# The experts' weights split into two parts one megabyte at a time

## The chip, the core and the metric

The kernel runs on one core of a Trainium2 chip. The metric is the device time of one execution in microseconds, as the median of several runs. TensorE multiplies, ScalarE (ACT) and VectorE (DVE) do element-wise work, GpSimd (POOL) a little of it, and SyncE (SP) issues most DMA transfers. Each engine works through its own instructions in a fixed order and waits on semaphores for the others.

## What is computed

A model of several layers runs over 256 tokens of 1024 channels, all in float32. The change touches only its last layer, a mixture of experts. A router picks two of eight experts for each token, and each expert is a gated feed-forward network.

```python
gates = jnp.sum(jax.nn.one_hot(top_idx, N_EXPERTS, dtype=jnp.float32) * top_w[..., None], axis=1)
for e in range(N_EXPERTS):
    y = swiglu_2(t, w_gate[e], w_up[e], w_down[e])       # (silu(t @ w_gate) * (t @ w_up)) @ w_down
    out = out + gates[:, e:e + 1] * y
```

The hidden width of an expert is 3584, so its three matrices hold 11 million weights, 44 MB. All eight hold 352 MB.

## The kernel before

TensorE takes the weights in a rounded 32-bit format, and one rounded copy is not exact enough. So every weight tile is split: ACT copies the raw float32 tile to `hi` in the rounded format (line 337), and DVE subtracts `hi` from the raw tile and writes the rest to `lo` (line 338). Each product is then made of matmuls with `hi` and matmuls with `lo`. The function `halves` does this for a tile of 128 partitions x 1024 columns (512 KB), which `load_half` has fetched (line 326, on SP's queue). All layers use it: the feed-forward, mixer and delta-net layers ahead of the experts get their weights through `stream`, and the experts call `chunk`, which handles two such tiles, 1 MB.

`hi` and `lo` come from two pools of three buffers each. A writer that wants a buffer waits until every reader of the tile that lay in it three tiles earlier is done: for `hi` that is DVE and TensorE, for `lo` TensorE. In the experts' stage the raw tiles rotate through four pools (`rawb`, `rawc`, `raw`, `rawe`) with 8 + 12 + 4 + 3 = 27 buffers of 512 KB. A few more buffers (`rawd`, `rawf`) serve once at the beginning, and the first eight tiles are fetched ahead, while the delta-net layer still computes. SP issues a transfer as soon as DVE has released the tile that lay in its buffer.

The function `short` runs the experts. A step is one of the seven blocks of 512 hidden columns of one expert, so there are 8 x 7 = 56 steps of six chunks. `gate_up` multiplies two chunks of gate weights and two of up weights, then makes silu times up (`sl`, line 1930 on ACT and 1931 on DVE). `down` of the step before multiplies two chunks of down weights after its own small matmuls (`x<-BOTH,sl`) and a split of their result (`hh`). For experts with at most 64 tokens (`FEW`), the high and the low part of the tokens lie side by side in one operand. They need two matmuls for each tile of 128 x 512 weights, eight in a chunk, and two extra matmuls a step that add the two sides (`gu<-both,BOTH`). The two experts with more tokens need three, twelve in a chunk. Six experts are of the first kind (42 steps), two of the second (14 steps: they run from about 1970 to 2090 us and from 2320 to 2430 us). Once an expert, `scatter` adds its output to the result (`yh`, `yl`, `ACC`), and `gather` collects the tokens of the next one or two experts (`XG`).

An automatic scheduler fixes the order on each engine when the kernel is built, from priorities in program order and its own estimate of times.

Of the kernel before, what the change touches and what calls it, by code (L numbers as in the profile page):

```python
# [9 lines left out]
F32 = mybir.dt.float32  # L10
# [47 lines left out]
NRB, NRC, NRD, NRE, NRF = 8, 12, 3, 3, 1  # L58
# [9 lines left out]
def _const_arrays():  # L68
# [31 lines left out]
    add("zero", np.zeros((P, P)))  # L100
# [149 lines left out]
class _K:  # L250
# [63 lines left out]
    def raw(self):  # L314
        if self.once:
            return self.T(self.once.pop(0), [P, 1024], "raw")
        self.nraw += 1
        return self.T(self.rawp[self.nraw % len(self.rawp)], [P, 1024], "raw")

    def load_half(self, ap, j, parts=1):  # L320
        if self.ahead:
            return self.ahead.pop(0)
        raw = self.raw()
        n = 1024 // parts
        for i in range(parts):
            self.nc.sync.dma_start(raw[:, i * n:i * n + n], ap[j, :, i * n:i * n + n])
        return raw

    def halves(self, raw, parts=1):

        nc = self.nc
        hi = self.T(self.hip, [P, 1024], "hi", F32R)
        lo = self.T(self.lop, [P, 1024], "lo", F32R)
        n = 1024 // parts
        for i in range(parts):
            c = slice(i * n, i * n + n)
            nc.scalar.activation(hi[:, c], raw[:, c], AF.Copy)  # L337
            nc.vector.tensor_tensor(lo[:, c], raw[:, c], hi[:, c].bitcast(F32), OP.subtract)  # L338
        return hi, lo
# [918 lines left out]
    def deltanet(self, outer):  # L1258
# [9 lines left out]
        with ExitStack() as st:  # L1268
# [158 lines left out]
            def feed():  # L1427
                for part, hg in _DN_ORDER:
                    yield from {"k": keys, "v": values, "z": zs}[part](hg)
                while not {("i", 0), ("i", 1)} <= done:  # L1430
                    yield 1.0

                first.close()
                self.ringb = outer.enter_context(tc.tile_pool(name="rawb", bufs=NRB, side="right"))
                self.once = [self.ringb] * NRB
                ahead.extend([self.load_half(self.A["moe"][0][j // 2], j % 2) for j in range(NRB)])
# [280 lines left out]
    def experts(self, base, HH, HL, ACC, RS, GT, key, st):  # L1717
# [50 lines left out]
        def gate_up(e, fb, XG, RX):  # L1768
            gu = []
            for m in range(2):  # L1770
                ps = self.T(self.psg, [P, 512], "gu")
                for q in range(2):
                    ch = self.chunk(self.A["moe"][e][fb * 6 + m * 2 + q])
                    for kk in range(4):
                        k = q * 4 + kk
                        wh, wl = ch[kk // 2]
                        c = slice((kk % 2) * 512, (kk % 2) * 512 + 512)
                        xh, xl = XG[:, 0, k, :], XG[:, 1, k, :]
                        self.mm(ps, ps, xh, wh[:, c], k == 0, False)
                        self.mm(ps, ps, xl, wh[:, c], False, False)  # L1780
                        self.mm(ps, ps, xh, wl[:, c], False, k == DT - 1)
                gu.append(ps)
# [5 lines left out]
        def down(e, fb, sl, ya, OT):  # L1788
# [6 lines left out]
            end = (e, fb) == (NE - 1, 6)  # L1795
            if end:
                raws = [self.load_half(self.A["moe"][e][fb * 6 + 4 + j // 2], j % 2, 2) for j in range(4)]
                self.gb, self.fin = self.raw(), self.raw()
                nc.sync.dma_start(self.gb, self.A["prow"][:, 24:24 + D].partition_broadcast(P))
            for n in range(2):  # L1800
                if not end:
                    ch = self.chunk(self.A["moe"][e][fb * 6 + 4 + n])
                for i in range(4):
                    c = slice((i % 2) * 512, (i % 2) * 512 + 512)
                    first, last = fb == 0 and i == 0, fb == 6 and i == 3
                    if end and i % 2 == 0:
                        w = self.halves(raws[2 * n + i // 2], 2)
                    wh, wl = w if end else ch[i // 2]
                    self.mm(ya[n], ya[n], hh[:, i, :], wh[:, c], first, False)
                    self.mm(ya[n], ya[n], hl[:, i, :], wh[:, c], False, False)  # L1810
                    self.mm(ya[n], ya[n], hh[:, i, :], wl[:, c], False, last)
# [31 lines left out]
    def short(self, HH, HL, ACC, RS, keyp, keyl, GTp, BOTH, where, st):  # L1843
# [16 lines left out]
        def gather(es):  # L1860
# [3 lines left out]
            for t in range(2):  # L1864
                for u, e in enumerate(es):
                    nc.vector.tensor_scalar(OH[:, t, u, :], self.c("iota"), keyp[:, t, e:e + 1], None, OP.is_equal)
                    nc.vector.tensor_scalar(OL[:, t, u, :], self.c("iota") if FEW[e] else self.c("zero"),
                                            keyl[:, t, e:e + 1] if FEW[e] else 1.0, None, OP.is_equal)
# [40 lines left out]
        def gate_up(e, fb, XG, RX):  # L1909
            gu = []  # L1910
            for m in range(2):
                ps = self.T(self.psg, [P, 512], "gu")
                for q in range(2):
                    ch = self.chunk(where(e)[fb * 6 + m * 2 + q])
                    for kk in range(4):
                        k = q * 4 + kk
                        wh, wl = ch[kk // 2]
                        c = slice((kk % 2) * 512, (kk % 2) * 512 + 512)
                        self.mm(ps, ps, XG[:, 0, k, :], wh[:, c], k == 0, False)
                        if not FEW[e]:  # L1920
                            self.mm(ps, ps, XG[:, 1, k, :], wh[:, c], False, False)
                        self.mm(ps, ps, XG[:, 0, k, :], wl[:, c], False, k == DT - 1)
# [11 lines left out]
        def down(e, fb, sl, ya, OT):  # L1934
# [13 lines left out]
            end = (e, fb) == (NE - 1, 6)  # L1948
            if end:
                raws = [self.load_half(where(e)[fb * 6 + 4 + j // 2], j % 2, 2) for j in range(4)]  # L1950
                self.gb, self.fin = self.raw(), self.raw()
                nc.sync.dma_start(self.gb, self.A["prow"][:, 24:24 + D].partition_broadcast(P))
            for n in range(2):
                if not end:
                    ch = self.chunk(where(e)[fb * 6 + 4 + n])
                for i in range(4):
                    c = slice((i % 2) * 512, (i % 2) * 512 + 512)
                    first, last = fb == 0 and i == 0, fb == 6 and i == 3
                    if end and i % 2 == 0:
                        w = self.halves(raws[2 * n + i // 2], 2)  # L1960
                    wh, wl = w if end else ch[i // 2]
                    self.mm(ya[n], ya[n], hh[:, i, :], wh[:, c], first, False)
                    if not FEW[e]:
                        self.mm(ya[n], ya[n], hl[:, i, :], wh[:, c], False, False)
                    self.mm(ya[n], ya[n], hh[:, i, :], wl[:, c], False, last)
# [94 lines left out]
    def build(self):  # L2060
        nc, tc = self.nc, self.tc
        with ExitStack() as st:
# [7 lines left out]
            ring = pool("raw", 4, side="right")  # L2070
            self.nraw, self.rawp, self.once, self.ahead = -1, [ring], [], []
            self.hip = pool("hi", 3, side="right")
            self.lop = pool("lo", 3, side="right")
# [56 lines left out]
            ringe = pool("rawe", NRE)  # L2130
            self.nraw, self.rawp = -1, [ringb] * NRB + [ringc] * NRC + [ring] * 4 + [ringe] * NRE
            self.once, self.ahead = rest + [ring] * 4 + [ringe] * NRE, ahead
# [21 lines left out]
```

## Time and profile before

| | us |
|---|---|
| median of 3 runs | 2569.28 (2568.91 to 2570.13) |
| profiled execution, its own time | 2570.35 |
| its span, first to last instruction | 2568.6 |
| DVE lo (line 338), all 1128 | 1344.0 busy, mean 1221 ns |
| ACT hi (line 337), all 1128 | 1167.7 busy, mean 1054 ns |
| DMA in the span | 603 MB, mean 235 GB/s |

Busy time of an instruction in the rows runs from its start to its end. On DVE and ACT the next one can start a little before the end of the one in front, so the cost of one among many is the distance from start to start. A matmul takes 0.39 us from start to end where the next one starts 0.23 us later. In a row of the timeline, several instructions of one kind are merged; the bracket gives the idle time of the engine before them and what ended it.

### The profile page before, as it was taken

What the parts mean: (1) busy time and instruction counts of PE and PEld (TensorE: products, weight loads), DVE (VectorE), ACT (ScalarE), POOL (GpSimd) and SP (SyncE); (2) the same over time, 40 slices, a digit from 0 to 9 for tenths busy, and PEclk for the clock granted to TensorE, in tenths of its full rate; (3) what the DMA queues carried; (4) which work ended last, traced back from release to release, by engine and by line L of the source; (5) the groups of instructions that cost most, each with busy time, mean ns of one, the idle gap of its engine ahead of it and who ended that gap; (6) DMA issues with size and microseconds to landing.
All of it is one profiled execution on the core that took longest, in us unless ns stands there. A gap on an engine that the chain in (4) does not pass through costs nothing. (4 is left out here: it accounts for less than half of the span.)

```text
span 2568.6 us, 44854 instructions
## 1 busy us (share of the span) xinstructions
PE 2499.9 (97%) x16795; PEld 2195.2 (85%) x16795; DVE 1981.9 (77%) x2663; ACT 1615.1 (63%) x2260; POOL 88.4 (3%) x87
## 2 busy tenths in 40 slices
PE   8999999999999999999999999899999999999997
PEld 8999899999999899999999998666667876677764
DVE  7657566666667667666765786799999899999897
ACT  5445464444445365454544675788888778887786
POOL 0003000000002100000000010000000000000000
PEclk9999999999999999999999999899999999999998
DMA  7554224555555223555555435899999999999993
GB/s 235 188 184 162 67 91 132 187 182 183 188 187 170 77 91 120 187 184 184 170 186 188 146 117 190 325 386 395 386 394 401 356 334 410 392 385 361 364 383 125
DMA packets 166914, 603.19 MB, mean 235 GB/s; under 512 B 18736, under 2 KB 19264, under 8 KB 166688
## 3 DMA queue, kind: packets, MB, share of 16 engines
q1 hardware_dynamic: 165792, 596.92, 65.1%
q0 software_dynamic: 896, 3.33, 0.4%
q8 instruction: 133, 2.18, 0.3%
q14 instruction: 93, 0.76, 0.1%
HBM read 597.03 MB, written 2.10 MB: 233 GB/s over the span
## 5 line engine op out<-in xcount | busy, mean ns | idle before, releaser
L338 DVE TENSOR_TENSOR lo<-raw,hi 128x1024 fp32r<-128x1024 f32 x1128 | 1344.0, 1221 | 362.1 <-ACT hi L337 358.3
L337 ACT ACTIVATE hi<-raw 128x1024 fp32r<-128x1024 f32 x1128 | 1167.7, 1054 | 710.8 <-issue 328.8
L265 PE MATMUL m<-xh,hi 128*128 128x256 f32 x1760 | 496.5, 282 | 9.7 <-ACT xh L366 9.2
L265 PE MATMUL m<-xh,lo 128*128 128x256 f32 x1760 | 496.6, 282 | 2.4 <-DVE lo L338 2.4
L265 PE MATMUL m<-xl,hi 128*128 128x256 f32 x1760 | 496.1, 282 | 1.8 <-DVE xl L367 1.8
L265 PE MATMUL gu<-lo,XG 128*128 128x512 f32 x896 | 393.4, 441 | 14.4 <-DVE lo L338 10.9
L265 PE MATMUL gu<-hi,XG 128*128 128x512 f32 x1120 | 403.6, 397 | 0.4 <-ACT hi L337 0.4
L265 PEld LDWEIGHTS m<-xh,hi 128*128 128x128 f32 x1760 | 334.4, 190 | 10.3 <-ACT xh L366 9.6
L265 PEld LDWEIGHTS m<-xh,lo 128*128 128x128 f32 x1760 | 334.2, 190 | 3.2 <-DVE lo L338 3.2
L265 PEld LDWEIGHTS m<-xl,hi 128*128 128x128 f32 x1760 | 334.2, 190 | 2.4 <-DVE xl L367 2.4
L265 PEld LDWEIGHTS gu<-lo,XG 128*128 128x128 f32 x896 | 169.0, 189 | 137.9 <-DVE lo L338 98.6
L265 PEld LDWEIGHTS gu<-hi,XG 128*128 128x128 f32 x1120 | 211.8, 189 | 48.5 <-issue 10.1
L265 PE MATMUL mm<-hl,hi 128*128 128x256 f32 x880 | 248.4, 282 | 0.0
L265 PE MATMUL mm<-hh,lo 128*128 128x256 f32 x880 | 248.4, 282 | 0.0
L265 PE MATMUL mm<-hh,hi 128*128 128x256 f32 x880 | 247.8, 282 | 0.0
L265 PE MATMUL mm<-xh,hi 128*128 128x256 f32 x832 | 240.0, 289 | 6.0 <-DVE x L1134 3.1
L265 PE MATMUL mm<-xl,hi 128*128 128x256 f32 x832 | 238.8, 287 | 0.0
L265 PE MATMUL mm<-xh,lo 128*128 128x256 f32 x832 | 237.3, 285 | 0.1
L265 PE MATMUL y<-lo,hh 128*128 128x512 f32 x448 | 184.7, 418 | 6.6 <-DVE lo L338 4.5
L265 PE MATMUL y<-hi,hh 128*128 128x512 f32 x448 | 179.5, 406 | 1.8 <-DVE hh L364 1.8
L265 PEld LDWEIGHTS mm<-hl,hi 128*128 128x128 f32 x880 | 168.4, 191 | 0.0
L265 PEld LDWEIGHTS mm<-hh,lo 128*128 128x128 f32 x880 | 168.4, 191 | 0.0
(585 smaller groups left out, 3382.5 us busy)
## 6 DMA issues: line engine op xcount, KB each, us to landing
raw<-in_moe SPq DMA_DIRECT2D x668, 512.0 KB, 6.2
raw<-in_ffn SPq DMA_DIRECT2D x330, 512.0 KB, 3.5
raw<-in_win SPq DMA_DIRECT2D x56, 512.0 KB, 3.5
raw<-in_dnin SPq DMA_DIRECT2D x32, 512.0 KB, 3.5
raw<-in_wout SPq DMA_DIRECT2D x16, 512.0 KB, 3.5
raw<-in_pin SPq DMA_DIRECT2D x8, 512.0 KB, 3.5
raw<-in_dnout SPq DMA_DIRECT2D x8, 512.0 KB, 3.5
raw<-in_moe SPq DMA_DIRECT2D x8, 256.0 KB, 5.9
```

Of the source, the lines that this page charges most:

```text
L265: ins = self.nc.tensor.matmul(out, lhsT=lhsT, rhs=rhs, start=start, stop=stop)
L337: nc.scalar.activation(hi[:, c], raw[:, c], AF.Copy)
L338: nc.vector.tensor_tensor(lo[:, c], raw[:, c], hi[:, c].bitcast(F32), OP.subtract)
```

## The change

The stream layers keep tiles of 1024 columns, but `hi` and `lo` of such a tile now lie side by side in one buffer of 2048 columns, from one pool `hl` of three. The experts go by a whole chunk. A raw tile (a "room") has 2048 columns, still filled by two transfers of 512 KB. ACT and DVE take it in one instruction each of 2048 columns. In the experts' stage `hi` and `lo` each have 2048 columns, and both come in turn from five buffers (three of `hl`, two of a new pool `hl2`). The raw rooms become 4 + 5 of 1 MB, and the four 512 KB buffers of the old ring serve as two more rooms, which ACT and DVE still take as two tiles of 1024 columns each. That makes 11 rooms, or 22 tiles of 512 KB. The very last two chunks are still split in pieces of 512 columns. The order of the small matmuls is as before. A constant of zeros is dropped (it gave way to the constant -1 in a comparison that never holds).

```diff
-NRB, NRC, NRD, NRE, NRF = 8, 12, 3, 3, 1
+NRB, NRC, NRD, NRF, NHL = 4, 5, 1, 1, 2
-    def halves(self, raw, parts=1):
+    def halves(self, raw):
-        hi = self.T(self.hip, [P, 1024], "hi", F32R)
-        lo = self.T(self.lop, [P, 1024], "lo", F32R)
+        t = self.T(self.hlp, [P, 2048], "hl", F32R)
+        hi, lo = t[:, 0:1024], t[:, 1024:]
+    def room(self):
+        ...
+        if pool is self.ring:
+            return [self.raw(), self.raw()]
+        return [self.T(pool, [P, 2048], "wide")]
+    def wide(self, room, parts=1):
+        nc = self.nc
+        self.npart += 2
+        hi, lo = [self.T(self.parts[(self.npart + i) % len(self.parts)], [P, 2048], "hl", F32R) for i in range(2)]
+        o = 0
+        for src in room:
+            w = src.shape[1]
+            n = w // parts
+            for i in range(0, w, n):
+                c = slice(o + i, o + i + n)
+                nc.scalar.activation(hi[:, c], src[:, i:i + n], AF.Copy)
+                nc.vector.tensor_tensor(lo[:, c], src[:, i:i + n], hi[:, c].bitcast(F32), OP.subtract)
+            o += w
+        return [(hi[:, i:i + 512], lo[:, i:i + 512]) for i in range(0, 2048, 512)]
...
-                    ch = self.chunk(where(e)[fb * 6 + m * 2 + q])
-                    for kk in range(4):
+                    for kk, (wh, wl) in enumerate(self.wide(self.load_wide(where(e)[fb * 6 + m * 2 + q]))):
...
-            self.hip = pool("hi", 3, side="right")
-            self.lop = pool("lo", 3, side="right")
+            self.hlp = pool("hl", 3, side="right")
...
-            ringe = pool("rawe", NRE)
-            self.nraw, self.rawp = -1, [ringb] * NRB + [ringc] * NRC + [ring] * 4 + [ringe] * NRE
+            self.npart, self.parts = -2, [self.hlp] * 3 + [pool("hl2", NHL)] * NHL
+            self.nroom, self.rooms = -1, [ringb] * NRB + [ringc] * NRC + [ring] * 2
```

## Rows read from the trace of the kernel before

**Rows 1.** The page: busy time of each engine, and the rate of the 40 slices.
```profile
PE 2499.9 (97%) x16795; PEld 2195.2 (85%) x16795; DVE 1981.9 (77%) x2663; ACT 1615.1 (63%) x2260; POOL 88.4 (3%) x87
...
GB/s 235 188 184 162 67 91 132 187 182 183 188 187 170 77 91 120 187 184 184 170 186 188 146 117 190 325 386 395 386 394 401 356 334 410 392 385 361 364 383 125
```
**Rows 2.** Busy time in stretches: stretch, length, engines (instructions), PEclk, DMA share, GB/s.
```profile
0.00:1560.00 1560.00, 1542.08 (x12574) 1498.79 (x12574) 1056.11 (x1637) 809.38 (x1279) 81.16 (x78) 1.00 0.49 158
1700.00:1825.00 125.00, 121.50 (x520) 84.43 (x519) 122.11 (x131) 107.95 (x130) 0.00 (x0) 1.00 1.01 395
1890.00:1960.00 70.00, 68.62 (x274) 46.26 (x273) 68.11 (x66) 62.43 (x71) 0.00 (x0) 1.00 1.03 411
2000.00:2050.00 50.00, 50.00 (x229) 40.76 (x228) 43.44 (x41) 38.05 (x42) 0.00 (x0) 1.00 0.99 363
```
**Rows 3.** Waits from 1700 to 1900 us: who for whom, us, times, longest.
```profile
PEld gu L265 <- DVE lo L338: 26.6, 57, 0.8
ACT hi L337 <- PE y L265: 11.7, 19, 2.3
ACT hi L337 <- PE gu L265: 7.9, 12, 2.0
DVE lo L338 <- ACT hi L337: 4.3, 10, 0.7
```
**Rows 4.** DVE's timeline over one step of an expert with few tokens.
```profile
1786.57 0.41 DVE L364 TENSOR_TENSOR hh<-x,hh 128x256 fp32r<-128x256 f32 x1
1786.90 6.92 DVE L338 TENSOR_TENSOR lo<-raw,hi 128x1024 fp32r<-128x1024 f32 x6
1794.21 1.23 DVE L338 TENSOR_TENSOR lo<-raw,hi 128x1024 fp32r<-128x1024 f32 x1 [0.39 <-ACT hi L337]
1795.36 0.75 DVE L1931 SCALAR_TENSOR_TENSOR sl<-gu,RX,sl 128x512 f32<-128x512 f32 x1
1796.02 5.76 DVE L338 TENSOR_TENSOR lo<-raw,hi 128x1024 fp32r<-128x1024 f32 x5
1801.69 0.41 DVE L364 TENSOR_TENSOR hh<-x,hh 128x256 fp32r<-128x256 f32 x1
```
**Rows 5.** Busy time in two whole steps, early and late, and one with a scatter.
```profile
1780.23:1795.36 15.13, 14.77 (x59) 9.80 (x59) 14.74 (x16) 13.57 (x16) 0.00 (x0) 1.00 1.03 413
2145.57:2160.83 15.26, 14.87 (x58) 9.53 (x58) 14.79 (x16) 13.25 (x16) 0.00 (x0) 1.00 1.03 414
1746.66:1765.11 18.45, 16.80 (x66) 11.19 (x67) 18.45 (x22) 14.56 (x18) 0.00 (x0) 1.00 0.99 379
```
**Rows 6.** DVE's timeline: two neighbouring instructions of 512 columns in a scatter.
```profile
1754.26 0.68 DVE L364 TENSOR_TENSOR yl<-y,yh 128x512 fp32r<-128x512 f32 x1
1754.86 0.74 DVE L1979 SCALAR_TENSOR_TENSOR ACC<-x,GTp,ACC 128x512 f32<-128x512 f32 x1
```
**Rows 7.** ACT's timeline in the step of rows 4.
```profile
1788.94 1.06 ACT L337 ACTIVATE hi<-raw 128x1024 fp32r<-128x1024 f32 x1 [0.41 <-PE gu L265]
1789.91 0.58 ACT L1926 ACTIVATE both<-gu 128x512 f32<-128x512 f32 x1
1790.38 1.99 ACT L337 ACTIVATE hi<-raw 128x1024 fp32r<-128x1024 f32 x2
1792.54 0.69 ACT L1930 ACTIVATE sl<-gu,RX 128x512 f32<-128x512 f32 x1 [0.17 <-PE gu L265]
```
**Rows 8.** TensorE's timeline in that step: the matmuls beside the chunks' own.
```profile
1791.48 1.02 PE L265 MATMUL gu<-both,BOTH 128*128 128x512 f32 x2
...
1796.32 1.00 PE L265 MATMUL x<-BOTH,sl 128*128 128x64 f32 x8
```
**Rows 9.** SP's waits from 1690 to 1960 us.
```profile
SPq L326 <- DVE lo L338: 139.9, 180, 2.5
```
**Rows 10.** ACT's timeline at the first expert's start and at the end.
```profile
1628.71 0.60 ACT L1888 ACTIVATE XG<-x 128x512 fp32r<-128x512 f32 x1 [10.30 <-PE x L265]
...
2548.56 1.15 ACT L337 ACTIVATE hi<-raw 128x512 fp32r<-128x512 f32 x2 [1.73 <-PE y L265]
```

More of the change, by code (lines that the diff above doesn't have):

```diff
@@ L314, in raw @@
     def raw(self):
[L315 to L318, printed above, removed]
+        return self.T(self.ring, [P, 1024], "raw")
     def load_half(self, ap, j, parts=1):
-        if self.ahead:
-            return self.ahead.pop(0)
         raw = self.raw()
@@ L1435, in feed @@
                 self.once = [self.ringb] * NRB
-                ahead.extend([self.load_half(self.A["moe"][0][j // 2], j % 2) for j in range(NRB)])
+                ahead.extend([self.load_wide(self.A["moe"][0][j]) for j in range(NRB)])
                 while ys[3] is None:
@@ L1795, in down @@
             end = (e, fb) == (NE - 1, 6)
+            raws = [self.load_wide(self.A["moe"][e][fb * 6 + 4 + n], 1 + end) for n in range(2)]
             if end:
-                raws = [self.load_half(self.A["moe"][e][fb * 6 + 4 + j // 2], j % 2, 2) for j in range(4)]
                 self.gb, self.fin = self.raw(), self.raw()
@@ L1800, in down @@
             for n in range(2):
[L1801 to L1804, printed above, removed]
+                for i, (wh, wl) in enumerate(self.wide(raws[n], 4 if end else 1)):
                     first, last = fb == 0 and i == 0, fb == 6 and i == 3
[L1806 to L1811, printed above, removed]
+                    self.mm(ya[n], ya[n], hh[:, i, :], wh, first, False)
+                    self.mm(ya[n], ya[n], hl[:, i, :], wh, False, False)
+                    self.mm(ya[n], ya[n], hh[:, i, :], wl, False, last)
             if fb == 6:
@@ L1948, in down @@
             end = (e, fb) == (NE - 1, 6)
+            raws = [self.load_wide(where(e)[fb * 6 + 4 + n], 1 + end) for n in range(2)]
             if end:
-                raws = [self.load_half(where(e)[fb * 6 + 4 + j // 2], j % 2, 2) for j in range(4)]
                 self.gb, self.fin = self.raw(), self.raw()
@@ L1953, in down @@
             for n in range(2):
[L1954 to L1957, printed above, removed]
+                for i, (wh, wl) in enumerate(self.wide(raws[n], 4 if end else 1)):
                     first, last = fb == 0 and i == 0, fb == 6 and i == 3
[L1959 to L1962, printed above, removed]
+                    self.mm(ya[n], ya[n], hh[:, i, :], wh, first, False)
                     if not FEW[e]:
-                        self.mm(ya[n], ya[n], hl[:, i, :], wh[:, c], False, False)
-                    self.mm(ya[n], ya[n], hh[:, i, :], wl[:, c], False, last)
+                        self.mm(ya[n], ya[n], hl[:, i, :], wh, False, False)
+                    self.mm(ya[n], ya[n], hh[:, i, :], wl, False, last)
             if fb == 6:
@@ L2069, in build @@
             self.xp = pool("xp", 1, stx)
[L2070 to L2073 removed]
+            ring = self.ring = pool("raw", 4, side="right")
+            self.nroom, self.once, self.ahead = -1, [], []
+            self.hlp = pool("hl", 3, side="right")
             self.cparts = []
```

48 lines of the change are left out of this document (27 added, 21 removed).

## The prediction

> **What bounds the kernel now.** I read the page first and then the same columns by stretch, because the page's 97% for TensorE and 77% for DVE are means over stages with different limits [rows 1]. Up to 1560 us TensorE is busy 1542 of 1560 us and DVE only 68%: the stream layers are TensorE's [rows 2]. From 1625 us on the experts run, and two kinds alternate there. In the two experts with many tokens TensorE has no gap at all (50.00 of 50 us) and DVE has slack (43.44) [rows 2]. In the six with few tokens DVE is busy 122.11 of 125 us, TensorE's weight loads wait for `lo` (26.6 us of 200), and DVE waits little (4.3 us) [rows 2, 3]. TensorE's 97% there is matmuls that wait in the pipe, not work. So DVE sets the time of 42 of the 56 steps, TensorE that of 14.
>
> One step shows what DVE does [rows 4]. From sl to sl it takes 15.13 us [rows 5]. Five `lo` take 5.76 us with the last one at 1.22, so one costs (5.76 - 1.22) / 4 = 1.135 us from start to start. hh costs 1786.90 - 1786.57 = 0.33, sl 1796.02 - 1795.36 = 0.66. The work is 12 x 1.135 + 0.33 + 0.66 = 14.61 us, and the other 0.5 us is a gap. After six `lo` the next could start at 1786.90 + 6 x 1.135 = 1793.71 and starts at 1794.21, because ACT's `hi` comes late. That `hi` had waited 0.41 us for TensorE to release its buffer, and then had both and sl in its way [rows 7]. Of the 42 steps 24 repeat this pattern: 12 before the first many-token expert at 15.1 us (gap 0.5) and 12 after it at 15.27 us (gap 0.65) [rows 5]. In a step with a scatter DVE is busy throughout, 18.45 of 18.45 us [rows 5].
>
> **The change part by part.** *Fewer, wider instructions on DVE.* The cost that doesn't grow with the width follows from two widths. An instruction of 512 columns costs 1754.86 - 1754.26 = 0.60 us from start to start [rows 6], one of 1024 columns 1.135 [rows 4]; 512 columns more cost 0.535, so 0.065 us is fixed and 2048 columns cost 1.135 + 1.07 = 2.205 us. A merged pair saves 0.065. Of the 336 chunks, 274 come as one tile: 60 fall to the two rooms of the old ring (4 + 9 first loads hold two of them, and 29 turns of 11 rooms hold 58) and two are the last. So of the 252 chunks of few-token steps about 252 x 274 / 336 = 206 are merged, and 206 x 0.065 = 13.4 us lies on the path, as DVE is the bound there. In the 14 TensorE-bound steps and in ACT it buys nothing: TensorE's work covers it.
>
> By the Trainium skill, "VectorE: DVE Perf Modes", section "The TRN2 errata", a float32 `tensor_tensor` of N columns takes (N + 151) / 0.96 ns, which is 1224 ns at 1024, as long as one lasts here; a merged pair would save 157 ns and the sum would be 206 x 0.157 = 32 us. The rows speak against it as a price in a row: neighbours overlap, so what counts is the distance from start to start.
>
> *Fewer stalls between the three engines.* Before, a writer needed the buffer of three half chunks back. Now `hi` and `lo` share five buffers in turn, so `hi` of chunk n takes the buffer of `lo` of chunk n-3, and `lo` of n that of `hi` of n-2. I check whether DVE must wait. Let D be the end of a `lo` on DVE; they follow at 2.2 us. TensorE's eight matmuls follow each other at 0.23 us, and most of them wait for `lo`, so TensorE is done with a chunk about 1.75 us after D. DVE wants the buffer 2.2 us after D: slack 0.45. The two matmuls of both last 1.02 us and the eight of x 1.00 [rows 8]; less the 0.16 by which a matmul outlasts the distance to the next (0.39 and 0.23) they delay what follows by 0.86 and 0.84. They fall to different chunks. The first makes TensorE done with the chunk behind it at 2.16 instead of 1.75 after D (0.86 less the gap of 0.45), still ahead of 2.2. The second falls where DVE does sl, which gives 0.66 more. ACT's `hi` of 2048 columns takes at most the 1.99 us of two neighbours now, and both costs 1790.38 - 1789.91 = 0.47 in front of it [rows 7]. It can start 1.75 us after D(n-3), at the latest 2.22, ends by 4.2 and is wanted at 4.4. So no wait is left in a clean step, though twice by only 0.1 to 0.2 us, and the gap goes: 12 x 0.5 + 12 x 0.65 = 13.8 us. Bounds 0 and 15.8 (2 us for gaps in the other 18 steps); I take 13.8, as the sum of waits is positive in every place.
>
> *Steps with gather and scatter.* There, small copies of ACT and DVE must now queue behind instructions of about 2 us instead of 1.1, while TensorE waits for their PSUM buffers. No row shows this cost. The nearest is ACT's longest wait for TensorE, 2.3 us [rows 3]; some ten such places give between 2 us gained (five buffers reach further than three) and 10 us lost. I take 3 lost, near zero, since the DVE-bound scatter step of rows 5 has no gap to lengthen now.
>
> *Start and end.* ACT lies idle for 10.3 us before the first expert, and could use it to fill more buffers; at the end its last `hi` waits 1.73 us for TensorE, which five buffers avoid [rows 10]. Together 0 to 5 us; I take 2, as TensorE works on beside both.
>
> *The transfers.* They stay 512 KB each and 22 tiles of buffer replace 27. SP waits for DVE, not for the memory [rows 9]. But a clean step now moves 6.29 MB in 15.13 us, 416 GB/s, while the DMA gives 411 over 70 us at a share of 1.03 [rows 2]: it runs at its limit and full buffers make up the difference. A step of 15.13 - 0.5 - 0.33 = 14.3 us asks for 440. That drains 30 GB/s x 14.3 us = 0.43 MB a step. Six steps drain 2.6 of 11.5 MB, scatter and gather refill it, and with them an expert takes some 108 us for 44 MB, 408 GB/s. So I cost the transfers at nothing, with full buffers as the cover. If that cover is gone, a step costs 6.29 MB / 411 GB/s = 15.3 us. *The stream layers* keep their instructions, and TensorE's 1542 of 1560 us hides a buffer that comes free one matmul later: 0, at most 2 either way.
>
> **The sum.** 13.4 + 13.8 + 2 - 3 = 26 us off the profiled execution's 2570.35 us gives 2544. The median of the runs lies 1.1 us below that execution, so 2543. With all terms at their good ends 13.4 + 15.8 + 5 + 2 + 2 = 38, so 2531; with all at their bad ends 13.4 - 10 - 2 = 1, so 2568.
>
> **The rivals.** *Only the overhead goes.* The gap of 0.5 us is replaced by another of the same size, as two of the margins above are 0.1 to 0.2 us: 13.4 + 2 - 3 = 12 off, 2557. For it speaks that ACT still does both, sl and hh in between.
>
> *The transfers become the bound.* The buffers run empty and clean steps cost 15.3 us, no less than now: 2567, give or take 5. For it: the DMA is at its limit in clean steps, and the store falls from 27 to 22 tiles. Against it: the mean of an expert, 408, is below 411, and SP waits for buffers all the time. The Trainium skill, "DMA: Bandwidth & Descriptors", section "Where 436 GB/s comes from", puts the ceiling at 435; by that a step couldn't be under 14.5 us either, so the page agrees that the buffers must bridge.
>
> *Slower: TensorE holds the buffers.* If both and x fall to one chunk, TensorE is done with it 1.75 + 0.86 + 0.85 - 0.45 = 3.0 us after D, and DVE's next but one `lo` starts 0.8 us late. From 0.83 us a step (0.33 + 0.5) on, the gain is eaten. With a second such place in the hh split the stall is about 1.1 us, 0.3 us a step worse than now, 42 x 0.3 = 12 us: 2582. Against it: the order of rows 8 keeps them apart by 4.8 us, more than two chunks.
>
> *The page's price.* Instructions don't overlap when wide, or the fixed cost is 157 ns: 26 + 32 - 13 = 45 off, 2524. Overlap shows in every row, so little speaks for it.
>
> *It doesn't do what it says.* It can't fail wholly, but 60 chunks stay in tiles of 1024; that is in the sum.
>
> **How the numbers follow.** Forecast 2543 with its own range 2531 to 2553: 0.62. Only the overhead, 2553 to 2563: 0.16. Transfers or no net gain, 2564 to 2574: 0.08. TensorE holds the buffers, 2575 to 2595: 0.08. The page's price, 2515 to 2531: 0.06. The range 2531 to 2563 holds the first two, 0.78. A measurement of this kernel can tell about 0.2%, 5 us, from no change: faster 0.62 + 0.16 + 0.06 = 0.84, same 0.08, slower 0.08.
>
> **What would show it.** DVE's 128x2048 rows: 274 in the experts, 2.2 us from start to start. Clean steps from sl to sl: 14.2 to 14.4 us; 14.8 would mean that only the overhead went, 15.3 with ACT waiting for raw tiles that the DMA is the bound, over 15.3 with DVE waiting for TensorE that the buffers are. Many-token steps stay at 17.3 us and the start of the experts at about 1625 us. The forecast is wrong if ACT or DVE wait for TensorE in few-token steps by more than 0.3 us a step.

## The result and the profile after

| | us | ratio to before |
|---|---|---|
| before, median | 2569.7 | |
| after, median of 4 runs (2602.96 to 2610.42) | 2608.2 | 1.0146 (1.0133 to 1.0158) |
| after, profiled execution, its span | 2610.42, 2608.6 | |

The change makes the kernel 1.5% slower. Forecast were 2543 us and a range up to 2563. Between the two profiled executions lie 2610.42 - 2570.35 = 40.1 us. I place them with one landmark of the experts' stage, DVE's 56 `sl` instructions. The first starts at 1642.3 us before and at 1670.4 after, so 28.1 us are lost ahead of the experts' steady work. From the first to the last it is 897.9 us before and 908.0 after, 10.1 lost. What comes behind the last takes 1.8 us more.

The page's costliest groups, after (busy us, mean ns of one, idle before):

```profile
L329 DVE TENSOR_TENSOR hl<-raw,hl 128x1024 fp32r<-128x1024 f32 x452 | 554.4, 1228 | 340.0 <-ACT hl L328 339.2
L366 DVE TENSOR_TENSOR hl<-wide,hl 128x2048 fp32r<-128x2048 f32 (+1 forms) x282 | 623.9, 2241 | 56.0 <-issue 18.1
L365 ACT ACTIVATE hl<-wide 128x2048 fp32r<-128x2048 f32 (+1 forms) x282 | 524.0, 1878 | 103.1 <-PE y L264 46.9
```

The wide instructions are there: 282 less the 8 pieces of 512 columns at the end are the 274 forecast.

The next table is the best view of the experts, and the rest of this text returns to it. It has one stretch for each kernel, from the first `sl` to the last (stretch, length, engines with instructions, granted clock, DMA share, GB/s): before, then after.

```profile
1642.30:2540.20 897.90, 875.21 (x3680) 623.51 (x3680) 853.26 (x860) 749.15 (x862) 0.00 (x0) 1.00 0.97 371
```
```profile
1670.40:2578.40 908.00, 851.65 (x3677) 648.77 (x3676) 832.52 (x592) 709.47 (x594) 0.00 (x0) 0.98 0.96 370
```

DVE's work fell by 853.26 - 832.52 = 20.7 us, as meant. Its idle time rose from 44.6 to 75.5 us, by 30.9. The difference is the 10 us. Before, no single wait of DVE in this stretch was over 1.5 us. After there are ten, and they add up to 32.7 us (the shortest, of 1.502 us, is left out where the expectation of e9 says 9 with 31 us).

The sum hides where the time goes. The 41 steps with few tokens between these two `sl` take 649.5 us before and 652.3 after: DVE works 18.7 us less in them and idles 21.5 us more. The 14 with many tokens take 248.4 us before and 255.8 after, 7.4 us more. TensorE sets their time, and it stands still for 7.0 us there instead of 1.4. These 14 steps, in two stretches, before and then after:

```profile
1954.60:2080.50 125.90, 125.61 (x571) 101.36 (x572) 113.94 (x119) 94.98 (x105) 0.00 (x0) 1.00 0.97 356
2306.20:2428.70 122.50, 121.41 (x530) 96.09 (x530) 110.51 (x106) 94.70 (x101) 0.00 (x0) 1.00 0.98 366
```
```profile
1987.20:2117.90 130.70, 127.37 (x581) 102.81 (x580) 113.99 (x84) 92.86 (x73) 0.00 (x0) 1.00 0.95 357
2341.20:2466.30 125.10, 121.40 (x529) 96.44 (x530) 108.47 (x72) 88.73 (x68) 0.00 (x0) 1.00 0.94 352
```

In after, TensorE's gaps there are thirteen waits of 0.1 to 0.9 us for `hi`, `lo`, `hh` and `sl` from ACT and DVE.

One of the ten long waits, on DVE (start, length, operation, count, idle before it and its cause). It begins in a step with a scatter; [rows 6] are two instructions of such a step before.

```profile
1781.08 1.40 DVE L1990 SCALAR_TENSOR_TENSOR ACC<-x,GTp,ACC 128x512 f32<-128x512 f32 x2
1782.40 4.48 DVE L366 TENSOR_TENSOR hl<-wide,hl 128x2048 fp32r<-128x2048 f32 x2
1786.80 1.40 DVE L1990 SCALAR_TENSOR_TENSOR ACC<-x,GTp,ACC 128x512 f32<-128x512 f32 x2
1788.12 2.28 DVE L366 TENSOR_TENSOR hl<-wide,hl 128x2048 fp32r<-128x2048 f32 x1
1790.32 0.74 DVE L1948 SCALAR_TENSOR_TENSOR sl<-gu,RX,sl 128x512 f32<-128x512 f32 x1
1790.98 0.41 DVE L393 TENSOR_TENSOR hh<-x,hh 128x256 fp32r<-128x256 f32 x1
1796.22 2.29 DVE L366 TENSOR_TENSOR hl<-wide,hl 128x2048 fp32r<-128x2048 f32 x1 [4.82 <-PE y L264]
```

TensorE at the same time:

```profile
1787.60 1.10 PE L264 MATMUL x<-BOTH,sl 128*128 128x64 f32 x8 [0.97 <-DVE ACC L1990]
1788.63 0.50 PE L264 MATMUL gu<-hl,XG 128*128 128x512 f32 x1
1791.12 1.97 PE L264 MATMUL x<-BOTH,sl 128*128 128x64 f32 x8 [1.99 <-DVE sl L1948]
1792.85 5.96 PE L264 MATMUL y<-hl,hh 128*128 128x512 f32 x16
```

Read it in order of time. Two small results that TensorE needs, ACC (which frees a PSUM buffer) and `sl`, stand on DVE behind `lo` instructions of 2.2 us, once behind two of them. TensorE waits 0.97 us for the one, before the first x, and 1.99 us for the other, before the x of the next step. Meanwhile ACT and DVE have already split both chunks of down weights. Those fill four of the five buffers. The matmuls that would empty them (y) need `hh` of the first x, whose low part stands on DVE behind the same `lo` and `sl`, and in TensorE's order they also come behind the x of the next step. So DVE runs out of buffers and waits 4.82 us. On top of that TensorE, which has just stood still, gets half its clock for the y matmuls (1.2 of 2.4 GHz):

```profile
1790.98:1796.22 5.24, 5.10 (x16) 4.43 (x17) 0.42 (x3) 0.00 (x0) 0.00 (x0) 0.50 0.74 292
```

The step that begins with this `sl` takes 19.8 us and the same one of the next expert 19.6; before, both took 15.1. Of the ten long waits the profile puts three down to y, like this one, and one to ACT; for six it names no releaser ("issue"). The wide kernel also has clean steps close to those that I forecast. Two of them, and an undisturbed stretch with many tokens:

```profile
2178.84:2193.50 14.66, 13.74 (x59) 9.87 (x58) 14.29 (x9) 12.39 (x10) 0.00 (x0) 1.00 1.02 408
2193.50:2208.00 14.50, 13.68 (x59) 9.90 (x57) 14.43 (x10) 13.23 (x12) 0.00 (x0) 1.00 1.03 409
2030.00:2080.00 50.00, 50.00 (x223) 40.45 (x222) 44.23 (x27) 36.66 (x28) 0.00 (x0) 1.00 0.96 357
```

The larger loss lies where I expected nothing, in the stream layers. I follow it with ACT's splits: the n-th split weight tile is the same tile in both kernels. How much later than before it starts, for several kernels (the runs named e are below):

| weight tile, its time before | 81, 243 us | 111, 432 us | 231, 774 us | 291, 1056 us | 441, 1527 us | first `sl`, 1642 us |
|---|---|---|---|---|---|---|
| after | 2.6 | 9.6 | 10.9 | 18.9 | 20.2 | 28.1 |
| e1 joint | 3.3 | 6.0 | 6.2 | 16.8 | 18.1 | 20.2 |
| e9 | 3.4 | 8.5 | 8.7 | 14.2 | 17.8 | 25.7 |
| e10 | 0.9 | 1.7 | 1.9 | 7.8 | 8.7 | 15.3 |
| e11 | 2.7 | 5.6 | 7.0 | 9.4 | 11.0 | 17.8 |
| e12 | -0.8 | -1.0 | -2.2 | -2.8 | 1.2 | -0.2 |
| e13 | -1.8 | -1.3 | -2.5 | -0.5 | 4.4 | 5.6 |
| e14 | -1.3 | 0.6 | -0.6 | -0.4 | 2.7 | 4.0 |
| e8 moved | 1.2 | 3.1 | 7.1 | 7.2 | 13.8 | 17.1 |

After loses in two places, the two mixer layers (243 to 432 and 774 to 1056 us), and next to nothing in the long feed-forward stretches between them. Both mixers by stretch, before and then after:

```profile
230.00:345.00 115.00, 114.95 (x830) 100.58 (x829) 77.57 (x119) 54.86 (x92) 16.02 (x11) 1.00 0.28 91
830.00:1040.00 210.00, 206.54 (x1549) 187.74 (x1548) 144.27 (x259) 105.18 (x189) 14.22 (x13) 0.99 0.32 102
```
```profile
230.00:345.00 115.00, 113.05 (x788) 99.57 (x787) 73.53 (x113) 52.54 (x86) 15.59 (x11) 0.94 0.28 88
830.00:1040.00 210.00, 202.38 (x1476) 182.92 (x1475) 141.40 (x254) 103.31 (x186) 21.75 (x15) 0.97 0.29 93
```

TensorE stands still 1.9 and 4.2 us longer, and its mean granted clock is 0.94 instead of 1.00 and 0.97 instead of 0.99. At 115 and 210 us that is another 6.9 and 4.2 us, an estimate from these rows. Together 8.8 and 8.4, about what the table shows (7.0 and 8.0); the second stretch holds not quite the same work, as after is 11 us late there. In the first mixer TensorE's standstill is one wait, in after only. By the profile it isn't a wait for weights but for a result of the mixer itself (`wA`); the second mixer has one more of the same length:

```profile
PE mm L264 <- ACT wA L706: 2.0, 1, 2.0
```

ACT's wait for TensorE to give a buffer back, in the first of these stretches, before and after:

```profile
ACT hi L337 <- PE mm L265: 16.6, 9, 3.7
```
```profile
ACT hl L328 <- PE mm L264: 29.7, 11, 5.9
```

### The profile page after: what moved, and what is told of

Read it like the earlier page. It is cut to its first block, busy times and chain, and to the rows that moved or that the text cites. A ratio compares the mean times of both kernels' runs of the same rounds, so it can differ in the third digit from the quotient of the medians.

```text
span 2608.6 us, 43951 instructions
## 1 busy us (share of the span) xinstructions
PE 2493.2 (96%) x16795; PEld 2236.1 (86%) x16795; DVE 1962.6 (75%) x2389; ACT 1576.5 (60%) x1986; POOL 94.7 (4%) x87
## 5 line engine op out<-in xcount | busy, mean ns | idle before, releaser
L328 ACT ACTIVATE hl<-raw 128x1024 fp32r<-128x1024 f32 x452 | 478.4, 1060 | 620.2 <-issue 333.2
L329 DVE TENSOR_TENSOR hl<-raw,hl 128x1024 fp32r<-128x1024 f32 x452 | 554.4, 1228 | 340.0 <-ACT hl L328 339.2
L366 DVE TENSOR_TENSOR hl<-wide,hl 128x2048 fp32r<-128x2048 f32 (+1 forms) x282 | 623.9, 2241 | 56.0 <-issue 18.1
L264 PE MATMUL m<-xh,hl 128*128 128x256 f32 x3520 | 630.6, 281 | 9.9 <-ACT xh L395 8.1
L365 ACT ACTIVATE hl<-wide 128x2048 fp32r<-128x2048 f32 (+1 forms) x282 | 524.0, 1878 | 103.1 <-PE y L264 46.9
L264 PE MATMUL gu<-hl,XG 128*128 128x512 f32 x2016 | 534.1, 409 | 29.9 <-DVE hl L366 18.9
L264 PEld LDWEIGHTS m<-xh,hl 128*128 128x128 f32 x3520 | 542.3, 189 | 11.0 <-ACT xh L395 8.5
L264 PEld LDWEIGHTS gu<-hl,XG 128*128 128x128 f32 x2016 | 371.5, 189 | 161.9 <-DVE hl L366 56.9
L264 PE MATMUL m<-xl,hl 128*128 128x256 f32 x1760 | 495.0, 282 | 2.2 <-DVE xl L396 2.2
L264 PE MATMUL mm<-xh,hl 128*128 128x256 f32 x1664 | 337.4, 292 | 12.8 <-ACT wA L706 3.9
L366 DVE TENSOR_TENSOR hl<-raw,hl 128x1024 fp32r<-128x1024 f32 x120 | 140.6, 1220 | 12.0 <-issue 7.6
L365 ACT ACTIVATE hl<-raw 128x1024 fp32r<-128x1024 f32 x120 | 120.5, 1054 | 23.2 <-PE y L264 13.2
```

Of the source, the lines that this page charges most:

```text
L264: ins = self.nc.tensor.matmul(out, lhsT=lhsT, rhs=rhs, start=start, stop=stop)
L328: nc.scalar.activation(hi, raw, AF.Copy)
L329: nc.vector.tensor_tensor(lo, raw, hi.bitcast(F32), OP.subtract)
L365: nc.scalar.activation(hi[:, c], src[:, i:i + n], AF.Copy)
L366: nc.vector.tensor_tensor(lo[:, c], src[:, i:i + n], hi[:, c].bitcast(F32), OP.subtract)
```

## The experiments

Two changes are suspected: the joint buffer of `hi` and `lo` in the stream layers, and the width of the experts' instructions. No kernel below leaves out any of the computation. All medians in one view (us; the ratio to before, with its interval; first `sl` and first to last `sl` are of the one profiled execution of each):

| run | median | ratio | first sl | first to last |
|---|---|---|---|---|
| before | 2569.7 to 2572.8 | | 1642.3 | 897.9 |
| after | 2608.2 | 1.0146 (1.0133 to 1.0158) | 1670.4 | 908.0 |
| e1_joint | 2600.4 | 1.0115 (1.0094 to 1.0137) | 1662.5 | 909.9 |
| e2_separate | 2604.1 | 1.0126 (1.0109 to 1.0143) | 1662.2 | 914.6 |
| e3_seven_buffers | 2602.4 | 1.0118 (1.0101 to 1.0135) | 1669.2 | 904.1 |
| e4_narrow | 2588.6 | 1.0068 (1.0052 to 1.0085) | 1661.5 | 899.0 |
| e5_order_kept | 2612.2 | 1.0153 (1.0131 to 1.0175) | 1669.4 | 912.9 |
| e6_kept_and_separate | 2592.3 | 1.0076 (1.0059 to 1.0093) | 1645.0 | 917.3 |
| e7_five_narrow | 2567.6 | 0.9985 (0.9975 to 0.9996) | 1645.2 | 891.6 |
| e8_moved | 2587.7 | 1.0062 (1.0045 to 1.0079) | 1659.4 | 898.2 |
| e9_only_narrow | 2599.0 | 1.0117 (1.0100 to 1.0134) | 1668.0 | 901.0 |
| e10_narrow_dve | 2622.7 | 1.0212 (1.0195 to 1.0229) | 1657.6 | 923.2 |
| e11_narrow_act | 2621.2 | 1.0208 (1.0190 to 1.0225) | 1660.1 | 921.2 |
| e12_both_undone | 2566.8 | 0.9987 (0.9977 to 0.9997) | 1642.1 | 894.0 |
| e13_separate_at_place | 2576.9 | 1.0023 (1.0010 to 1.0036) | 1647.9 | 902.3 |
| e14_six_singles | 2580.4 | 1.0033 (1.0020 to 1.0047) | 1646.3 | 905.6 |

### The joint buffer alone

The kernel before with this edit, and nothing wider:

```diff
-        hi = self.T(self.hip, [P, 1024], "hi", F32R)
-        lo = self.T(self.lop, [P, 1024], "lo", F32R)
+        t = self.T(self.hlp, [P, 2048], "hl", F32R)
+        hi, lo = t[:, 0:1024], t[:, 1024:]
```

> The kernel before with one edit: hi and lo of a 1024-column tile share one buffer of a pool of three, in the stream layers and in the experts; nothing is wider. Theory A (the joint buffer alone makes the scheduler order the two mixers otherwise): the experts start some 20 us later than before, about 2590 us. Rival B (the time before the experts is lost to the wide rooms that are fetched ahead): no loss, 2570 us.

Measured 2600.4 us, with 20.2 us lost by the first `sl` and 12 in the experts, where this kernel shares the joint buffers too (clean steps of 15.5 us). So the edit that I costed at nothing makes about half of the loss by itself, 20.2 of some 40 us, ahead of the experts. Up to the experts it has TensorE's order of the kernel after, instruction by instruction. Against before, 881 of the first 12,398 matmuls stand elsewhere in that order.

### Undoing it in the changed kernel

e2 takes hi and lo apart again, in two pools placed elsewhere in the memory; e3 adds two buffers in the experts, for two rooms less; e4 is e2 with instructions of 1024 columns:

```diff
-            self.hlp = pool("hl", 3, side="right")
+            self.hip = pool("hi", 3, stx)
+            self.lop = pool("lo", 3, stx)
```

> The changed kernel, but the stream layers keep separate pools of three for hi and lo, in memory that is given back before the experts; the experts then have five buffers of 2048 columns from one pool. Theory A: the 20 us in the mixers come back, the experts stay as in the changed kernel, about 2588 us. Rival B: no more than 3 us come back, 2605 us.

> As e2_separate, with seven buffers for hi and lo in turn instead of five and two raw rooms fewer (nine). Theory C (in steps with scatter or gather TensorE waits for a small DVE result that is queued behind an expert's lo, and five buffers are full before it comes): two more buffers give back 15 to 25 us of e2_separate, about 2565 to 2573 us. Rival D (small copies queue behind instructions that are twice as long, whatever the buffers): as e2_separate, 2588 us. Rival E (fewer raw rooms starve ACT): slower than e2_separate, with ACT waiting for DMA.

> As e2_separate, with instructions of 1024 columns on ACT and DVE; rooms and buffers stay at 2048 columns. Theory C: the stalls of steps with scatter and gather stay and the 13 us of merged instructions are lost, about 2600 us. Rival D: the stalls go, about 2577 us.

The streams got back only 6.6 us of the 20.2 in e2 (4 and 7 in the others), which spoke against the joint buffer until e8 explained it. So e2's time (2604.1) is the one of its rival, e3's is near e2's, as its rival D says, and e4's (2588.6) lies between its two theories. Within the three, the streams are alike and the experts can be compared. Seven buffers instead of five take 10.5 us off the first-to-last time (914.6 to 904.1), though eleven waits over 1.5 us stay, 25.1 us in all. Narrow instructions in the same buffers take off 15.6 us (to 899.0), with four such waits, 15.2 us. But e3 starts its first `sl` 7.0 us later than e2, and by the medians the buffers bring 1.7 us and the width 15.5. So the width does more than the number of buffers.

### The order of x and y

In after, six of the 42 groups of x matmuls stand on TensorE ahead of the y of the step before, in before none. e5 puts a dependence that keeps x behind y; e6 is e5 with the stream layers' separate pools where before has them:

```diff
+            behind(self.mm(ps, p4[:, i, n], sl[:, i * P:i * P + P], BOTH[:, n], True, True))
+            lasty[0] = self.mm(ya[n], ya[n], hh[:, i, :], wl, False, last)
```

> The changed kernel with one more constraint for the scheduler: on TensorE the small matmuls x<-BOTH,sl of a step come behind the last down product y of the step before, as they do in the kernel before (in the changed kernel they stand ahead of it in six steps). Theory C' (the long stalls of DVE, 31 us in all, come from that order: TensorE waits for sl, sl stands on DVE behind lo, and the buffers that DVE and ACT wait for are held by the down products behind): some 25 us less than the changed kernel, about 2583 us, and no DVE wait over 3 us. Rival D (width): as the changed kernel, 2608 us.

> As e5_order_kept, and the stream layers keep hi and lo in separate pools of three at the place that they have in the kernel before; the experts' five buffers are new memory, paid for with three raw rooms (eight instead of eleven). Theory A (joint buffers cost the stream layers some 20 us): 2583 - 18 = 2565 us. Rival E (eight rooms starve ACT): above 2575 us with ACT waiting for DMA.

e5 is no faster (2612.2), and ten waits over 1.5 us remain, of 28.9 us, though none is over 3.5. In after a long wait follows each of the six exchanged places. In e5 the wait at the first of these places is still 3.45 us, and there y waits for `hh`:

```profile
1790.42 6.45 PE L264 MATMUL y<-hl,hh 128*128 128x512 f32 x16 [2.31 <-DVE hh L393]
```

So the exchanged order isn't the cause by itself. e6 shows the streams within 1.6 us of before, up to the last mark: at their own place, separate pools give the whole stream loss back. Its time (2592.3 against 2565 expected) is lost in the experts. Beside e13, the same kernel with the order left free, the fixed order costs 15 us; beside after, in e5, 4 us.

### More buffers without width, and the place

e7 is before with five buffers each for hi and lo in the experts. e8 is before with its two pools at e2's place and nothing else:

```diff
+            self.hip, self.lop = pool("hi2", 5), pool("lo2", 5)
```
```diff
-            self.hip = pool("hi", 3, side="right")
-            self.lop = pool("lo", 3, side="right")
+            self.hip = pool("hi", 3, stx)
+            self.lop = pool("lo", 3, stx)
```

> The kernel before with five buffers of 1024 columns each for hi and lo in the experts instead of three, new memory, paid for with 10 raw tiles of 512 KB (17 instead of 27); nothing is wider. If the gap of 0.5 to 0.65 us in clean steps is a matter of buffers alone: 24 steps lose it, about 2556 us. Rival: the gap stays, 2570 us.

> The kernel before, with the pools for hi and lo of the stream layers at another place in memory (released before the experts, which have three new buffers each); nothing else changes, and the order of the instructions up to the experts is the same. Theory F (where the weights lie sets how long a weight load takes, 188 or 192 ns): the stream layers take 6 to 13 us more, about 2580 us. Rival: no change, 2570 us.

e7 is a little faster than before, 0.9985, and far from the 2556 us expected. Its clean steps take 14.6 us in the first experts (before 15.1), so the gap of 0.5 us that I saw does go with more buffers. Later they stay at 15.3. e8 runs before's order of instructions and is 16 us slower. It explains e2 to e4, which have before's order on TensorE in the streams, too: e8 loses 13.8 us there, e2 13.6. The rows stand in the last section.

### One edit in the changed kernel

e9 cuts the experts' instructions to 1024 columns and leaves all else; e10 does it on DVE only, e11 on ACT only:

```diff
-            n = w // parts
+            n = min(w // parts, 1024)
```

> The changed kernel with one edit: the experts' instructions on ACT and DVE are at most 1024 columns wide again, the 1 MB rooms and the five shared buffers stay, and so does the joint buffer of the stream layers. Nothing is left out. Theory (width in the queue): a small result waits behind an instruction of at most 1.2 instead of 2.2 us, so the waits over 1.5 us on DVE fall from 9 with 31 us to 5 or fewer with under 16 us, first to last sl falls from 908 to 895 to 902 us, and the time from 2608 to 2594 to 2602; the first sl stays at 1670. Rival (the five shared buffers, not the width, cause the long waits): they stay above 25 us and the time is 2620 to 2630, as the 18 us of fixed cost come back on top.

> The changed kernel with only DVE's instructions of the experts in pieces of 1024 columns, ACT's stay at 2048. Nothing is left out. If the results that wait on DVE (ACC, hh's second part, sl) carry the loss, this brings all that e9_only_narrow brings or nearly so: 2594 to 2604. If ACT's queue carries it (both, hh's first part, sl's silu, yh), nothing comes back and the 18 us of DVE's fixed cost are added: 2615 to 2627. A lo of 1024 must also wait for all of a hi of 2048, about 1 us later than in e9_only_narrow, which could cost the late clean steps some tenths.

> The changed kernel with only ACT's instructions of the experts in pieces of 1024 columns, DVE's stay at 2048. Nothing is left out. If DVE's queue carries the loss: 2603 to 2610, as the changed kernel, with the long waits on DVE above 22 us. If ACT's carries it: 2580 to 2594, as the long waits go and DVE keeps its lower fixed cost.

e9 came out as the width theory has it: 2599.0, and five waits over 1.5 us with 16.4 us (under 16 were expected). From first to last `sl`:

```profile
1668.00:2569.00 901.00, 870.93 (x3675) 631.32 (x3673) 847.57 (x859) 724.48 (x861) 0.00 (x0) 0.98 0.97 373
```

DVE works 15.1 us longer than in after and idles 22.0 us less. e10 and e11 together fit neither theory. By its time e10 is where ACT's queue would carry the loss (2615 to 2627), but then e11 should have been at 2580 to 2594, and it took 2621.2. Both are slower than after, by 13 to 15 us, although each is one half of e9's edit. A split is a chain, ACT then DVE, and with unequal widths DVE waits for ACT in the late experts too. A step of e10 on DVE, then one of e11:

```profile
2147.62 4.74 DVE L368 TENSOR_TENSOR hl<-wide,hl 128x1024 fp32r<-128x1024 f32 x4 [1.06 <-ACT hl L365]
```
```profile
2148.98 2.29 DVE L369 TENSOR_TENSOR hl<-wide,hl 128x2048 fp32r<-128x2048 f32 x1 [1.03 <-ACT hl L367]
```

So they don't tell which engine's queue carries the loss, and that stays open. Beside it e10 shows how the stream loss is made up. It has after's order of TensorE in the streams, without a difference, and lost 8.7 us there instead of 20.2. Two stretches of the first mixer, of before, of after and of e10:

```profile
230.00:250.00 20.00, 19.95 (x164) 19.37 (x163) 20.00 (x28) 10.57 (x14) 7.06 (x3) 1.00 0.47 148
290.00:310.00 20.00, 20.00 (x154) 18.03 (x153) 11.51 (x21) 10.24 (x18) 3.14 (x3) 1.00 0.19 56
```
```profile
230.00:250.00 20.00, 18.05 (x129) 17.31 (x129) 19.96 (x28) 9.74 (x14) 4.66 (x3) 0.91 0.44 140
290.00:310.00 20.00, 20.00 (x118) 17.24 (x117) 7.53 (x13) 8.67 (x15) 2.76 (x2) 0.80 0.16 54
```
```profile
230.00:250.00 20.00, 18.05 (x140) 16.98 (x140) 19.96 (x28) 9.87 (x14) 4.46 (x3) 1.00 0.47 145
290.00:310.00 20.00, 20.00 (x153) 17.62 (x154) 9.83 (x17) 11.05 (x19) 2.76 (x2) 1.00 0.17 54
```

After and e10 make the same pause (18.05 of 20 us). In after the clock falls in both stretches (0.91 and 0.80), in e10 in neither. So the pauses come with the joint buffer, and what the clock adds differs between executions. By the clock records of the traces TensorE ran at 1.2 GHz for 6.8 us of the streams before, for 34.1 in after and for 6.8 in e10. Half of such a time is what it can cost, so I estimate from these times that the clock made 13.7 of after's 20.2 us and none of e10's 8.7. The other four kernels with a joint buffer and this order (e1, e5, e9, e11) lost 11.0 to 18.1 us there; less the same estimate all six come to 5.7 to 8.7. The four executions of e10 go the same way: the fastest, 2614.4 us, had a mean clock of 0.986, the slowest, 2627.1 us, 0.980. The profiled ones of e10 and e11 are the fastest of their four, 7 to 8 us below the median.

### Both undone, and each alone at the same place

e12 is the kernel after with separate pools at before's place and 1024 columns. What stays of the change are rooms of 1 MB (8 of them) and five shared buffers. e13 is e12 with 2048 columns. e14 is e13 with hi and lo in turn from one pool of six buffers of 1024 columns: the memory of the joint buffers, but two releases.

```diff
+            self.hip = pool("hi", 3, side="right")
+            self.lop = pool("lo", 3, side="right")
+            self.npart, self.parts = -2, [pool("hl2", 3 + NHL)] * (3 + NHL)
```

> The changed kernel with both suspected causes undone: the stream layers have separate buffers for hi and lo where the kernel before has them, and the experts' instructions are at most 1024 columns wide. What stays of the change: rooms of 1 MB (8 instead of 11), five shared buffers of 2048 columns. Nothing is left out. If the two causes are all there is: first sl at 1643 to 1646, first to last sl 893 to 902, time 2565 to 2575, as the kernel before. If a third cause is in the shared buffers or the rooms: above 2580.

> The changed kernel with one of the two suspected causes undone: the stream layers have separate buffers for hi and lo where the kernel before has them, the experts keep instructions of 2048 columns (five shared buffers, 8 rooms) and TensorE's order is left to the scheduler. Nothing is left out. If the two causes add, this is the changed kernel (2608) less the 20 to 26 us that the joint buffer costs before the first sl: first sl at 1643 to 1648, first to last sl 908 to 918, time 2582 to 2592. If the width alone costs nothing once the streams are right (the long waits being a result of the late start and the lower clock): below 2575.

> As e13_separate_at_place, but hi and lo of the stream layers come in turn from one pool of six buffers of 1024 columns: the same 24 KB at the same place as the joint buffer's three, each half with its own release. Nothing is left out. If it is the single release of both halves (with the order that the scheduler makes for it) that costs the 20 us: as e13 within 5 us, first sl at 1643 to 1650. If it is where hi and lo lie in the memory, side by side: first sl at 1656 to 1670 and a time of 2595 to 2610.

e12, e13, e9 and after are the four corners:

| median, us | 1024 columns | 2048 columns | width costs |
|---|---|---|---|
| separate buffers | 2566.8 (e12) | 2576.9 (e13) | 10.1 |
| joint buffer | 2599.0 (e9) | 2608.2 (after) | 9.2 |
| the joint buffer costs | 32.2 | 31.3 | |

The two add up. (By the ratios to before, each on its own chip, the width costs 9.3 and 7.5 us.) Together they are 41.4 us, and without them the kernel is as fast as before, or a touch faster (0.9987). The joint buffer costs more than the 20 to 26 us that I had put down for it, since e13 came in below the 2582 to 2592 us that I expected. 22.5 to 25.9 us of it come before the first `sl`, and 5.7 to 7.0 behind it. e12 and e13 also have fewer rooms than e9 and after, so these last 6 or 7 us are not the joint buffer's beyond doubt. Nor are 7 to 9 us between the last stream tiles and the first `sl`: e2 to e4, with separate buffers, lose 6.2 to 10.6 us there. e14 parts the release and keeps the memory: first `sl` at 1646.3. So the place isn't it. What costs is one tile for both halves, with one release, and the order that the scheduler makes for that. Which of these two it is stays open, as they always go together here: up to the experts every kernel with the joint buffer has after's order on TensorE and every kernel with two pools has before's, and e14's differs from before's at 69 of 12,398 places.

What the width does, from first to last `sl`, e12 and e13:

```profile
1642.10:2536.10 894.00, 868.47 (x3675) 621.39 (x3673) 849.04 (x858) 722.62 (x861) 0.00 (x0) 1.00 0.99 379
```
```profile
1647.90:2550.20 902.30, 844.49 (x3677) 643.49 (x3676) 834.29 (x615) 711.36 (x617) 0.00 (x0) 0.99 0.97 375
```

DVE works 14.8 us less and idles 23.0 us more (45.0 to 68.0), so this stretch is 8.3 us longer; from e9 to after it is 7.0. Much of that lies in the 14 steps with many tokens, which take 250.8 us in e12 and 254.9 in e13, 247.4 in e9 and 255.8 in after. The 41 others go from 643.2 to 647.4 and from 653.5 to 652.3. The width also changes the scheduler's order: x stands ahead of y in one place in e12 and in four in e13, in three in e9 and in six in after. No run changes the width and holds the order, so what the waiting behind wide instructions costs is not shown apart from the change of order.

## Why the prediction was wrong

**The stream layers keep their instructions: 0, at most 2 either way.** This step failed first. It cost 20.2 us by the end of the streams and 28.1 by the first `sl`. I took TensorE's 1542 busy of 1560 us [rows 2] as cover for a buffer that comes free one matmul later. A busy share is no cover: in the first mixer it was 114.95 of 115 us before, and yet TensorE stood still there after, for a small result of the mixer. I had also read "they keep their instructions" as "they keep their order". The order is made by a scheduler that sees the buffers, and 881 matmuls of the streams changed their place. The pauses in the two mixers are worth 6 us and the lower clock another 11, by the rows: the stretch was costed without the clock. How much the clock adds differs from execution to execution, as e10 shows, so the size of the 20.2 is in part luck; that it is far above 2 is not, as all six kernels with this order lost 8.7 or more.

**Steps with gather and scatter: 3 lost, bounds 2 gained and 10 lost.** The mechanism was named rightly (small results behind instructions of 2 us, TensorE waiting for their PSUM buffers), but the term was mis-sized. DVE's idle time grew by 23.0 us where the width alone differs (13.9 of it in steps with few tokens), and by 30.9 in after (21.5). I had bounded it by the longest wait in sight, 2.3 us [rows 3], in some ten places. But a late small result doesn't cost its own lateness. It stops TensorE, TensorE then keeps four of five buffers, and in the rows above the clock is at half: the longest of these waits are 3.5 to 4.8 us on DVE in e13 and after. That it is the waiting behind wide instructions and not the changed order is argued from the rows, as no run parts the two.

**Fewer, wider instructions: 13.4.** Right as a price. Two neighbours take 4.48 us and one 2.28, so 2.20 us from start to start against 2.205 forecast. DVE's work fell by 14.8 us between e12 and e13. By the Trainium skill, "VectorE: DVE Perf Modes", section "The TRN2 errata", one of 2048 columns takes (2048 + 151) / 0.96 = 2291 ns, and the trace agrees (2.28 to 2.29 us for one alone). The 157 ns that I worked out from this formula for a merged pair don't appear between neighbours (2 x 1.135 - 2.20 = 0.07 us), so that rival is out.

**No wait is left in a clean step: 13.8.** Wrong by most of it. There are clean steps of 14.50 and 14.66 us in after, against 14.2 to 14.4 forecast, so the buffers do what I worked out where nothing disturbs the pattern. But most others lie anywhere between 12.5 and 17 us, and the long waits come on top. In e12, where five buffers work with narrow instructions, the first-to-last time is 3.9 us better than before. The gap goes in the first experts (14.6 us) and stays later (15.3). The rows there point to another wait in order, which my recurrence left out, though no run tried it: `hh` on ACT waits for TensorE with the next `hi` behind it. The sign that I had named came, too: DVE's wide `lo` waited 25.2 us for TensorE in the experts, 0.2 before. ACT of e12, and DVE:

```profile
2148.44 0.38 ACT L392 ACTIVATE hh<-x 128x256 fp32r<-128x256 f32 x1 [1.65 <-PE y L264]
2153.31 0.60 ACT L1943 ACTIVATE both<-gu 128x512 f32<-128x512 f32 x1 [0.70 <-PE gu L264]
```
```profile
2154.89 2.36 DVE L366 TENSOR_TENSOR hl<-raw,hl 128x1024 fp32r<-128x1024 f32 x2 [0.36 <-ACT hl L365]
```

**Start and end: 2.** Not seen. Of the 28.1 us at the first `sl`, 7.9 arise between the last stream tiles and it, and the end is 1.8 us longer. I can't split those 7.9 us: e9, e10 and e11 show 6.6 to 7.9 there too, e2 to e4 6.2 to 10.6, e1 2.1, e13 and e14 1.2 and 1.3.

**The transfers: 0.** Right. Steps of 14.5 us ran at 408 and 409 GB/s, and in all of the experts DVE's waits for a transfer add up to 4.9 of its 75.5 idle us.

**Steps with many tokens: TensorE's work covers them, 17.3 us.** Wrong in the sum. Undisturbed ones stay at 17.2 us with TensorE at 50.00 of 50 us. But the 14 together take 7.4 us longer, 5.6 of them standstill of TensorE, and e9's 247.4 us show that this comes with the width. I had taken DVE's slack there as room, and left out that TensorE also waits for the small results.

Of the rivals, "TensorE holds the buffers" gave the right sign and, for the three long waits that the profile puts down to y, the right wait with 2582. Its cause, both and x in one chunk, is not what the rows show, and it knew nothing of the streams. The other three gave times at or below 2567.

## What to carry to other kernels

Price a wide instruction by what stands behind it in its engine's queue, not only by what it saves: here 15 us less work on DVE came with 23 us more idle time, and the steps that TensorE sets grew by 4 to 8 us. When two tiles are put into one buffer, or anything is changed that a scheduler sees, look at the order of the untouched stages too, and look for stages where TensorE's work is a chain of small dependent pieces, as there each pause can cost a spell at half clock on top. What helped a little here was more buffers at the old width (0.9985 and 0.9987).

## What the runs showed of the hardware

Where buffers lie in the on-chip memory can change the speed of TensorE. e8 differs from before in the place of hi and lo, and perhaps of pools opened behind them, with the same order in the streams, and is 16 us slower. In the same feed-forward stretch (1290 to 1390 us; busy us, mean ns) the weight loads take 188 ns before and 192 in e8, the matmuls 280 and 283, and TensorE, busy for all of the 100 us in both, gets through 855 and 836 of them:

```profile
L265 PE MATMUL m<-xl,hi 128*128 128x256 f32 x187 | 52.3, 280 | 0.0
L265 PEld LDWEIGHTS m<-xh,lo 128*128 128x128 f32 x186 | 35.0, 188 | 0.0
```
```profile
L265 PE MATMUL m<-xl,hi 128*128 128x256 f32 x215 | 60.8, 283 | 0.0
L265 PEld LDWEIGHTS m<-xh,lo 128*128 128x128 f32 x214 | 41.1, 192 | 0.0
```

Why the place matters isn't shown. The other surprise is told with e10: the same pause of TensorE was followed by a lower clock in one execution and not in the other.
